# All eight tiles of u computed in pairs of seven products, in turn with the first gate pairs

## The chip, the core and the metric

The kernel runs on one core of one Trainium2 chip. The metric is device time in microseconds of one execution. The kernel before took 785.49 us in the median of three runs (784.92 to 785.92); its profiled execution took 785.08 us, of which the profile's span, from the first to the last instruction, is 783.3 us.

## What is computed

One layer of an encoder trunk on 512 tokens of width 1024, in float32. The change lies in the middle of the first half, in the three lines on u, on the spatial mix and on the two gates:

```python
q, k, v, g, u, sv, a_ret, a_sgu = jnp.split(proj, list(np.cumsum(IN_SPLITS)[:-1]), axis=-1)
y_ret = _retention_branch(q, k, v, g, ret_decay_logit, w_ret_o)      # (o * silu(g)) @ w_ret_o
u = jax.nn.gelu(u)
sv = _layernorm(jax.nn.gelu(sv), sgu_ln_g, sgu_ln_b)
mixed = jnp.einsum('gpq,bnqgc->bnpgc', w_spatial, svc) + b_spatial.T[None, None, :, :, None]
y = u * mixed.reshape(B, S, SGU_W)                                   # then y @ w_sgu_o
merged = jax.nn.sigmoid(a_ret) * y_ret + jax.nn.sigmoid(a_sgu) * y_sgu
```

`u` and the two gates are products of the normalised input (1024 x 512) with 1024 columns of `w_in` each, `y_ret` and `y_sgu` end in a product with another 1024 x 1024 matrix. Each is eight tiles of 128 features by 512 tokens.

## The kernel before

**Numbers.** A float32 operand is split into a high part (a ScalarE copy that rounds, `copy`, L97) and a low part (a VectorE subtraction, `split`, L116), and a product of two operands is three TensorE matmuls: high by high, high by low, low by high (`mm3`, L291 to L293).

**Whole tiles and pairs.** A tile of 128 features can be made by `f_block`: eight 128 x 128 weight blocks, three matmuls of 512 columns each, 24 in all, into one PSUM bank. Its weights are one unit of 1024 columns ("blk"). Two tiles can also be made together by `Pair`: the two feature tiles, the two halves of the inner dimension and the two halves of the tokens form a 2 x 2 by 2 x 2 block product, which takes seven half-sized products in place of eight. Each product is twelve matmuls of 256 columns (L917), so a pair takes 84. Its weights are seven forms: three of the raw blocks as they are (`B11`, `B21`, `B22`) and four sums (`T1` to `T4`, L198 to L204). Each form is split like a block and holds one of nine slots (`w4`); a whole tile's weights hold two. The raw weights come by DMA from SyncE's queue into four `raw` tiles; a pair holds three of them (two loads and one tile of sums) until its last forms are split.

**The three parts of a pair.** `part1` issues four products. The first goes to bank 0, and ScalarE copies it to the output tile; the second goes to bank 1 and VectorE adds it (L938); the third goes to bank 2; the fourth accumulates into bank 0, on top of the first, so it may start only when ScalarE's copy of the first product is done. `part2` is one product more into bank 0, which needs the next such copy done, and `part3` two, one into bank 0 and one into bank 2. Between the parts stand other matmuls, which cover the copies. `part3` ends with the scaling by `rbc` (L962, L967) and the activation (L963, L968).

**The stages around the change.** The SGU's normalised operand ends at about 199 us with `row_sums`. Then: four tiles of u by `f_block`, each scaled on VectorE (L979) and through gelu on ScalarE (L980), with the layer norm of sv beside them (`sv_stats`, `sv_scale`, `sv_norm`); two pairs of u (`UW` = 4 is the tile where the pairs begin); then four rounds `j` of one gate pair (sigmoid, `gated_pair`), two tiles of the retention's output by `f_block`, the gating product (L1051) into `r`, and two `mix`es. A mix is four 128 x 128 matmuls (L1011), an affine step (L1019) and the product with u (L1027) on VectorE, and the split of the result into `yh`, `yl`. After that come four rounds of the second gate, whose whole tiles read `yh` and `yl`, and then `w_out` and the feed-forward part, which the change leaves alone.

**Order.** Each engine runs its instructions in a fixed order. A scheduler sets it when the program is built, from the order of the source and from `issue_after`, which puts a block's instructions behind a named instruction on the same engine. `w_get` decides how far the weights run ahead: it fills units until eight or ten slots are spoken for.

Of the kernel before, what the change touches and what calls it, by code (L numbers as in the profile page):

```python
# [15 lines left out]
P = 128  # L16
# [11 lines left out]
SV0, U0, GATE0, GATE1 = 24, 32, 40, 72  # L28
UW = 4
LOOK = 4  # L30
# [8 lines left out]
EARLY = 4  # L39
QK = (4, 0, 5, 1, 6, 2, 7, 3)  # L40
COUPLES = [(i, i + 1) for i in range(4, 20, 2)]

# [7 lines left out]
def tile_block(ctx: ExitStack, tc, xT, x, wall, par, cs, wsp, bsp, gpost, gffn, out):  # L50
# [74 lines left out]
    while i < NW:  # L125
        pair = [(f, i) for f in FORMS]
        if i == SV0:
# [149 lines left out]
    def w_get(look=LOOK):  # L277
# [10 lines left out]
        return w_ready.pop(i)  # L288

    def mm3(o, ah, al, bh, bl, start, stop, skip=False):  # L290
        nc.tensor.matmul(o, ah, bh, start=start, stop=False, skip_group_check=skip)  # L291
        nc.tensor.matmul(o, ah, bl, start=False, stop=False, skip_group_check=skip)  # L292
        nc.tensor.matmul(o, al, bh, start=False, stop=stop, skip_group_check=skip)  # L293

# [605 lines left out]
    class Pair:  # L900
# [9 lines left out]
        def product(self, b, act, first, w=None):  # L910
            wh, wl = w or w_get()
            o = self.b[b][:, T0]
            for k in range(4):
                c = slice(k * P, (k + 1) * P)
                h_, l_ = act(k)
                for n, (w_, a_) in enumerate(((wh, h_), (wh, l_), (wl, h_))):
                    self.last = nc.tensor.matmul(  # L917
                        o, w_[:, c], a_, start=first and k == n == 0, stop=k == 3 and n == 2,
                        skip_group_check=True,
                    )  # L920
            return self.two(o)

# [33 lines left out]
        def part3(self):  # L956
# [4 lines left out]
            else:  # L961
                v.tensor_mul(two(c0[:, T1]), o, two(self.scale[:, T1]))  # L962
                nc.scalar.activation(out=c0, in_=c0, func=self.func)  # L963
            o = self.product(2, self.s("S4"), False, self.w[1])
            v.tensor_sub(two(c1[:, T0]), o, two(c1[:, T0]))
            if self.scale is not None:
                v.tensor_mul(c1, c1, self.scale)  # L967
                nc.scalar.activation(out=c1, in_=c1, func=self.func)  # L968


    bst = lo64("bst", F32)
    nc.gpsimd.dma_start(bst, bsp.rearrange("g p -> (g p)")[None, :].to_broadcast([P, S]))
    uT, late = [], None
    U_HOMES = [lambda: lo64("u", F32), lambda: hi192("u", F32)] + [lambda: blk(n="u")] * 2 + [lambda: hi192("u", F32)] * 4
    for j in range(UW):
        with tc.issue_after(summed) if j == 0 else ExitStack():
            o = f_block(xh, xl, KD)
        u = U_HOMES.pop()()
        i = v.tensor_mul(two(u), in_turn(o), two(rbc)).ins  # L979
        g = nc.scalar.activation(out=u, in_=u, func=AF.Gelu_apprx_tanh).ins  # L980
        uT.append(u)
        with tc.issue_after(i):
            sv_stats(((0, 1), (2, 3), (), ())[j])
        if j == 1:
            sv_scale()
        if j > 1:
            with tc.issue_after(g):
                sv_norm(j - 2, range((NT, 2)[j - 2]))
    for j in range(UW // 2, KD // 2):
        p = Pair(AF.Gelu_apprx_tanh, lambda: U_HOMES.pop()(), None, rbc)  # L990
        p.part1()
        if late:
            late.part3()
        p.part2()
        late = p
        uT += p.t
        if j == UW // 2:
            with tc.issue_after(p.copied):
                sv_norm(1, range(2, NT))
    yh, yl = [], []  # L1000

    def mix(j):
# [7 lines left out]
        for t in range(NT):  # L1010
            nc.tensor.matmul(  # L1011
                o[:, t * P : (t + 1) * P],
# [3 lines left out]
                stop=True,  # L1016
            )
        m = tmp("mix")
# [7 lines left out]
        )  # L1026
        v.tensor_mul(uT[j], m, uT[j])  # L1027
        h_, l_ = blk(F32R, "yh"), blk(F32R, "yl")
        split(h_, l_, uT[j])
# [3 lines left out]

    def gated_pair(ah, al, late=None):

        p = Pair(AF.Sigmoid, lambda: tmp("sig"), None, rbc)
        with tc.issue_after(late.last.ins) if late else ExitStack():
            p.part1()
        if late:
            with tc.issue_after(p.last.ins):  # L1040
                late.part3()
        o = [f_block(ah, al, KD)]
# [3 lines left out]

    r = []
    for j in range(KD // 2):
        for o, t in gated_pair(ogh, ogl, late if j == 0 else None):
            b = (lo64("r", F32) if j == 0 else hi192("r", F32) if j < 3 else blk(n="r"))  # L1050
            v.tensor_mul(two(b), in_turn(o), two(t))  # L1051
            r.append(b)
        mix(2 * j)
        mix(2 * j + 1)
    mh, ml = [], []
# [605 lines left out]
```

## Time and profile before

| What | Value |
|---|---|
| median of three runs | 785.49 us |
| profiled execution | 785.08 us |
| its span | 783.3 us |
| TensorE, mean granted clock | 0.998 |
| from the first matmul of u to the first of the second gate | 199.34 to 325.38 us |
| the same stretch, ScalarE busy | 63.53 us of 126.04 |
| one table load on ScalarE there | 1.28 us |

A row of the timeline gives the start, the duration, the engine, the source line, the operation with output and inputs, and how many alike were merged. Durations of TensorE overlap, since its matmuls are pipelined: what one costs is the distance to the next start. The chain of waits lists the pieces of work that ended last, one behind the other, so its pieces on TensorE do not overlap. On ScalarE and VectorE too the next instruction of a row of like ones starts some 0.1 us before the one ahead has ended.

### The profile page before, as it was taken

How to read it: one execution, taken by the hardware profiler on the slowest of the kernel's cores; microseconds unless marked ns; L12 is line 12 of the kernel's file. 1: busy time of each engine (PE TensorE's matmuls, PEld its weight loads, DVE VectorE, ACT ScalarE, POOL GpSimd, SP SyncE). 2: the span in 40 equal slices, each digit the busy share in tenths (PEclk: the TensorE clock that was granted, in tenths of full speed). 3: DMA queues.
4: the chain of work that ended last, by engine and by line, in shares of the span. 5: the costliest groups of instructions: out<-in, count | busy, mean ns of one | idle time of the engine just before them, and what ended most of it. 6: DMA issues, size and time to landing. Idle time of an engine off the chain costs nothing.

```text
span 783.3 us, 13258 instructions
## 1 busy us (share of the span) xinstructions
PE 775.6 (99%) x5067; PEld 720.3 (92%) x5067; DVE 626.5 (80%) x1067; ACT 467.8 (60%) x848; POOL 104.0 (13%) x132
## 2 busy tenths in 40 slices
PE   9999999999999999999999999999999999999996
PEld 8888998998899999999998998999999998999996
DVE  7467887788786877867765679989999889877987
ACT  7555558689385544444444776657777578644542
POOL 0040001130012111032211200001111012200001
PEclk9999999999999999999999999999999999999999
DMA  8782224453123333223459111425555365632244
GB/s 293 260 266 88 81 82 162 108 133 126 55 106 108 108 108 108 106 84 108 138 161 344 57 69 39 122 108 141 141 149 149 108 196 114 170 114 108 108 162 162
DMA packets 35889, 104.78 MB, mean 134 GB/s; under 512 B 4401, under 2 KB 6321, under 8 KB 35825
## 3 DMA queue, kind: packets, MB, share of 16 engines
q1 hardware_dynamic: 27936, 87.81, 31.8%
q0 software_dynamic: 7024, 14.95, 9.0%
q10 hardware_dynamic: 864, 1.18, 0.4%
q8 instruction: 39, 0.64, 0.3%
q14 instruction: 26, 0.20, 0.1%
HBM read 91.34 MB, written 4.19 MB: 122 GB/s over the span
## 4 chain that ended last, share of the span: by engine, by line
PE 98%; DVE 1%; ACT 0%; POOLq 0%; issue 0%; POOL 0%; DVEq 0%
PE ps L917 22%; PE ps L291 13%; PE ps L293 13%; PE ps L292 13%; PE ps L1354 11%; PE ps L746 5%; PE ps L625 4%; PE ps L627 4%; PE ps L626 4%; PE ps L1089 2%; PE ps L1091 2%; PE ps L1090 2%; PE ps L1370 2%; PE ps L1011 1%; PE ps L411 1%; PE ps L393 0%
## 5 line engine op out<-in xcount | busy, mean ns | idle before, releaser
L116 DVE TENSOR_TENSOR wl<-raw,wh 128x1024 fp32r<-128x1024 f32 (+1 forms) x88 | 100.6, 1152 | 56.1 <-issue 20.6
L97 ACT ACTIVATE wf<-raw 128x512 fp32r<-128x512 f32 x126 | 75.6, 624 | 83.8 <-PE ps L292 37.1
L97 ACT ACTIVATE wh<-raw 128x1024 fp32r<-128x1024 f32 (+2 forms) x92 | 89.1, 981 | 28.9 <-DMA raw<-wall 15.5
L917 PE MATMUL ps<-sh,wf 128*128 128x256 f32 x576 | 105.3, 275 | 0.0
L116 DVE TENSOR_TENSOR wf<-raw,wf 128x512 fp32r<-128x512 f32 x126 | 93.3, 754 | 14.9 <-ACT wf L97 14.7
L917 PEld LDWEIGHTS ps<-sh,wf 128*128 128x128 f32 x576 | 91.7, 192 | 0.8 <-ACT u L97 0.2
L291 PE MATMUL ps<-h2h,wh 128*128 128x512 f32 (+1 forms) x256 | 90.7, 354 | 0.0
L293 PE MATMUL ps<-h2h,wl 128*128 128x512 f32 (+1 forms) x256 | 90.4, 353 | 0.0
L292 PE MATMUL ps<-h2l,wh 128*128 128x512 f32 (+1 forms) x256 | 90.4, 353 | 0.0
L917 PE MATMUL ps<-sl,wf 128*128 128x256 f32 x288 | 79.3, 275 | 0.0
L1354 PE MATMUL ps<-dh,fh 128*128 128x256 f32 x216 | 59.5, 276 | 0.0
L1354 PE MATMUL ps<-dh,fl 128*128 128x256 f32 x216 | 59.5, 275 | 0.0
L1354 PE MATMUL ps<-dl,fh 128*128 128x256 f32 x216 | 59.4, 275 | 0.0
L917 PEld LDWEIGHTS ps<-sl,wf 128*128 128x128 f32 x288 | 55.3, 192 | 0.4
L97 ACT ACTIVATE dh<-raw 128x768 fp32r<-128x768 f32 (+1 forms) x36 | 33.6, 950 | 33.5 <-DVE raw L224 17.6
L293 PEld LDWEIGHTS ps<-h2h,wl 128*128 128x128 f32 x256 | 48.6, 190 | 5.1
L291 PEld LDWEIGHTS ps<-h2h,wh 128*128 128x128 f32 x256 | 48.7, 190 | 4.5
L292 PEld LDWEIGHTS ps<-h2l,wh 128*128 128x128 f32 x256 | 48.7, 190 | 4.4
L627 PE MATMUL ps<-wh,xl 128*128 128x512 f32 x128 | 48.6, 379 | 0.0
L626 PE MATMUL ps<-wl,xh 128*128 128x512 f32 x128 | 48.5, 379 | 0.0
L625 PE MATMUL ps<-wh,xh 128*128 128x512 f32 x128 | 48.5, 380 | 0.0
L917 PE MATMUL ps<-xh,wf 128*128 128x256 f32 x240 | 43.8, 276 | 0.0
(343 smaller groups left out, 2185.8 us busy)
## 6 DMA issues: line engine op xcount, KB each, us to landing
raw<-wall SPq DMA_DIRECT2D x144, 512.0 KB, 3.6
x<-x SPq DMA_DIRECT2D x24, 256.0 KB, 5.9
fl<-gp POOLq DMA_DIRECT2D x12, 256.0 KB, 4.0
swap<-qkraw POOLq DMA_DIRECT2D x16, 128.0 KB, 4.3
x<-x POOLq DMA_DIRECT2D x8, 256.0 KB, 2.3
fl<-fs POOLq DMA_DIRECT2D x8, 256.0 KB, 3.3
xT<-xT SPq DMA_DIRECT2D x7, 256.0 KB, 5.5
xT<-xT POOLq DMA_DIRECT2D x4, 256.0 KB, 4.0
```

Source lines behind the costliest of these rows:

```text
L97: return nc.scalar.activation(out=o, in_=i, func=AF.Copy)
L116: low[0] = nc.vector.tensor_sub(lo, src, as32(hi)).ins
L291: nc.tensor.matmul(o, ah, bh, start=start, stop=False, skip_group_check=skip)
L292: nc.tensor.matmul(o, ah, bl, start=False, stop=False, skip_group_check=skip)
L293: nc.tensor.matmul(o, al, bh, start=False, stop=stop, skip_group_check=skip)
L625: nc.tensor.matmul(acc[t], xh[k][:, c], turns(wh[:, f]), start=k == 0, stop=False)
L626: nc.tensor.matmul(acc[t], xh[k][:, c], turns(wl[:, f]), start=False, stop=False)
L627: part_end[0] = nc.tensor.matmul(acc[t], xl[k][:, c], turns(wh[:, f]), start=False, stop=k == KD - 1)
L746: nc.tensor.matmul(bank[t], a_[:, c], turns(w_[:, f]), start=first and k == i == 0, stop=last and k == 3 and i == 2, skip_group_check=True,)
L917: self.last = nc.tensor.matmul(o, w_[:, c], a_, start=first and k == n == 0, stop=k == 3 and n == 2, skip_group_check=True,)
L1089: nc.tensor.matmul(o, ah, turns(bh), start=k == 0, stop=False)
L1354: nc.tensor.matmul(o, a_[:, c], turns(w_[:, f]), start=j == t == i == 0, stop=j == DP - 1 and i == 2 and n not in (M2, M3, M4), skip_group ...
```

## The change

The four whole tiles of u become two more pairs, so that u is four pairs, and the order of the whole stretch is written out in a table, `MIDDLE`. In it `W` is a whole tile of the retention's output, `U1`, `U2`, `U3` and `G1`, `G2`, `G3` are the three parts of a pair of u and of a gate pair, `UA` and `GA` their activations, `M` a mix without its split, and `Y` the split. Each step is issued behind the last matmul of the step ahead.

```diff
-UW = 4
+MIDDLE = [(i[:-1], int(i[-1])) for i in (
+    "W0 W1 U10 W2 U20 G10 U30 G20 U11 G30 W3 UA0 GA0 M0 M1 U21 G11 Y0 Y1 U31 G21 U12 G31 W4 UA1 GA1 M2 M3 U22 G12"
+    " Y2 Y3 U32 W5 G22 U13 G32 W6 UA2 GA2 M4 M5 U23 G13 U33 W7 UA3 Y4 Y5 G23 M6 M7 G33 GA3 Y6 Y7"
+).split()]
...
-        elif U0 + UW <= i < GATE0:
-            units += pair
-            i += 2
+        elif i == U0:
+            us, gs = ([[(f, k + n * m) for f in FORMS] for n in range(KD // 2)] for k, m in ((U0, 2), (GATE0, 4)))
+            ws = [("blk", GATE0 + 4 * (n // 2) + 2 + n % 2) for n in range(KD)]
+            for what, n in MIDDLE:
+                units += {"W": lambda: ws[n : n + 1], "U1": lambda: us[n][:4], "U2": lambda: us[n][4:],
+                          "G1": lambda: gs[n][:4], "G2": lambda: gs[n][4:]}.get(what, list)()
+            i = GATE0 + 2 * KD
...
                 v.tensor_mul(two(c0[:, T1]), o, two(self.scale[:, T1]))
-                nc.scalar.activation(out=c0, in_=c0, func=self.func)
+                if self.func:
+                    nc.scalar.activation(out=c0, in_=c0, func=self.func)
...
         v.tensor_mul(uT[j], m, uT[j])
+
+    def mixed(j):
         h_, l_ = blk(F32R, "yh"), blk(F32R, "yl")
         split(h_, l_, uT[j])
...
+    def whole(n):
+        o = f_block(ogh, ogl, KD)
+        r.append(lo64("r", F32) if n < 3 else hi192("r", F32) if n == 3 else blk(n="r"))
+        done = copy(two(r[n]), in_turn(o)).ins
+        if n < 2:
+            with tc.issue_after(low[0]):
+                sv_stats(((0, 1), (2, 3))[n])
+                if n:
+                    sv_scale()
+        if 0 < n < 5:
+            with tc.issue_after(done):
+                sv_norm((n - 1) // 2, range(NT)[:2] if n % 2 else range(NT)[2:])
+
+    def u_first(n):
+        us[n] = Pair(None, lambda: hi192("u", F32), None, rbc)
+        us[n].part1()
+
+    def u_acts(n):
+        for i, t in enumerate(us[n].t):
+            nc.scalar.activation(out=t, in_=t, func=AF.Gelu_apprx_tanh)
+            uT[2 * n + i] = t
+
+    def g_first(n):
+        gs[n] = Pair(None, lambda: tmp("sig"), None, rbc)
+        gs[n].part1()
+
+    def g_acts(n):
+        for i, t in enumerate(gs[n].t):
+            nc.scalar.activation(out=t, in_=t, func=AF.Sigmoid)
+            v.tensor_mul(r[2 * n + i], r[2 * n + i], t)
...
+    pe_last[0] = summed
+    for what, n in MIDDLE:
+        with tc.issue_after(pe_last[0]):
+            does[what](n)
```

A whole tile of the retention's output is now copied to `r` by ScalarE as it is, and the gate is multiplied in later, from SBUF. The second gate's pairs keep their old form. In the weights' layout all of u is now stored as pairs.

How the change moves instructions is shown at three places, in each engine's own order. The numbers in a name tell buffers apart: the last of them is the tile's own. In the changed kernel the same source lines have other numbers (L97 has become L100, L116 L119, L962 L972, L967 L978, L1019 L1005).

**ScalarE where a pair of u begins.** Before, the second pair of u (`ps_483_2484` is its bank 0). Its first copy is the last row here:

```order
L97 ACTIVATE u_467_2380<-ps_468_2381 128x256
L717 ACTIVATE sv_383_1912<-sv_383_1912,sshift_776,srstd_775 128x512
L97 ACTIVATE wf_476_2453<-raw_472_2400 128x512
L717 ACTIVATE sv_384_1913<-sv_384_1913,sshift_776,srstd_775 128x512
L97 ACTIVATE u_467_2380<-ps_468_2381 128x256
L97 ACTIVATE wf_477_2470<-raw_462_2343 128x512
L97 ACTIVATE wf_480_2477<-raw_478_2473 128x512
L97 ACTIVATE u_481_2482<-ps_483_2484 128x256
```

Of the change, the second pair (`ps_492_2567` is its bank 0, step `U11`):

```order
L1052 ACTIVATE u_455_2301<-u_455_2301 128x512
L100 ACTIVATE sig_477_2442<-ps_478_2443 128x256
L100 ACTIVATE wf_488_2558<-raw_473_2434 128x512
L1052 ACTIVATE u_456_2302<-u_456_2302 128x512
L100 ACTIVATE wf_489_2562<-raw_482_2462 128x512
L100 ACTIVATE u_490_2565<-ps_492_2567 128x256
```

The first copy of the new pair now stands behind both gelus of the pair before (`u_455_2301`, `u_456_2302`), and those wait for VectorE's scaling of that pair.

**ScalarE where the second gate begins.** Before, the last sigmoid of the first gate, and the first copy of the first pair of the second (`ps_637_3535` is its bank 0):

```order
L968 ACTIVATE sig_601_3310<-sig_601_3310 128x512
L97 ACTIVATE wf_621_3444<-raw_613_3385 128x512
L97 ACTIVATE wf_640_3538<-raw_610_3362 128x512
L97 ACTIVATE yh_628_3515<-u_481_2482 128x512
L97 ACTIVATE sig_635_3533<-ps_637_3535 128x256
```

Of the change (`ps_647_3667` is that bank):

```order
L100 ACTIVATE wf_634_3603<-raw_621_3491 128x512
L100 ACTIVATE yh_641_3657<-u_585_3248 128x512
L100 ACTIVATE wf_650_3670<-raw_618_3457 128x512
L1061 ACT_TABLE_LOAD
L1061 ACTIVATE sig_611_3435<-sig_611_3435 128x512
L100 ACTIVATE yh_643_3661<-u_586_3249 128x512
L1061 ACTIVATE sig_612_3436<-sig_612_3436 128x512
L100 ACTIVATE sig_645_3665<-ps_647_3667 128x256
```

A table load, both sigmoids of the last gate pair (`GA3`) and two splits of mixes have come directly ahead of that copy.

**VectorE at the same place.** Before, from the gating product of the last round to the addition in the second gate's first pair (L938):

```order
L1051 TENSOR_TENSOR r_624_3503<-ps_622_3447,sig_601_3310 128x512
L116 TENSOR_TENSOR wf_621_3444<-raw_613_3385,wf_621_3444 128x512
L1019 SCALAR_TENSOR_TENSOR mix_627_3512<-ps_626_3507,part_63,add_625_3505 128x512
L1005 SCALAR_TENSOR_TENSOR add_630_3519<-rws_382_1911,part_63,bst_443_2205 128x128
L1027 TENSOR_TENSOR u_481_2482<-mix_627_3512,u_481_2482 128x512
L1019 SCALAR_TENSOR_TENSOR mix_632_3526<-ps_631_3521,part_63,add_630_3519 128x512
L116 TENSOR_TENSOR wf_640_3538<-raw_610_3362,wf_640_3538 128x512
L116 TENSOR_TENSOR yl_629_3516<-u_481_2482,yh_628_3515 128x512
L1027 TENSOR_TENSOR u_482_2483<-mix_632_3526,u_482_2483 128x512
L938 TENSOR_TENSOR sig_635_3533<-ps_638_3536,sig_635_3533 128x256
```

Of the change, up to the scaling that the second sigmoid waits for (L978):

```order
L119 TENSOR_TENSOR wf_633_3599<-raw_617_3456,wf_633_3599 128x512
L1005 SCALAR_TENSOR_TENSOR mix_637_3613<-ps_636_3608,part_63,add_635_3606 128x512
L991 SCALAR_TENSOR_TENSOR add_638_3616<-rws_382_1911,part_63,bst_444_2213 128x128
L1013 TENSOR_TENSOR u_585_3248<-mix_637_3613,u_585_3248 128x512
L119 TENSOR_TENSOR wf_634_3603<-raw_621_3491,wf_634_3603 128x512
L1005 SCALAR_TENSOR_TENSOR mix_640_3623<-ps_639_3618,part_63,add_638_3616 128x512
L972 TENSOR_TENSOR sig_611_3435<-ps_613_3437,rbc_103_567 128x256
L1013 TENSOR_TENSOR u_586_3249<-mix_640_3623,u_586_3249 128x512
L976 TENSOR_TENSOR sig_612_3436<-ps_615_3439,sig_612_3436 128x256
L119 TENSOR_TENSOR yl_642_3658<-u_585_3248,yh_641_3657 128x512
L978 TENSOR_TENSOR sig_612_3436<-sig_612_3436,rbc_103_567 128x512
```

Ahead of them stand the low part of the first whole tile of the second gate (`wl_632_3582`), two splits of mixes (`yl_627_3572`, `yl_629_3576`) and a 128 x 256 subtraction (L963). The scalings of the last gate pair (L972, L976, L978) were done before the mixes in the old order, and now stand between and behind them.

More of the change, by code (lines that the diff above doesn't have):

```diff
@@ L920, in product @@
                     )
+            pe_last[0] = self.last.ins
             return self.two(o)
@@ L967, in part3 @@
                 v.tensor_mul(c1, c1, self.scale)
-                nc.scalar.activation(out=c1, in_=c1, func=self.func)
+                if self.func:
+                    nc.scalar.activation(out=c1, in_=c1, func=self.func)
     bst = lo64("bst", F32)
     nc.gpsimd.dma_start(bst, bsp.rearrange("g p -> (g p)")[None, :].to_broadcast([P, S]))
[L973 to L999, printed above, removed]
+    uT = {}
     yh, yl = [], []
@@ L1031, in mix, with gated_pair @@
         yl.append(l_)
-    def gated_pair(ah, al, late=None):
+    def gated_pair(ah, al):
         p = Pair(AF.Sigmoid, lambda: tmp("sig"), None, rbc)
[L1037 to L1041, printed above, removed]
+        p.part1()
         o = [f_block(ah, al, KD)]
@@ L1045, in gated_pair @@
         return zip(o, p.t)
[L1047 to L1054, printed above, removed]
+    r, us, gs = [], {}, {}
+    def whole(n):
[24 more added lines that the diff above has]
+            v.tensor_mul(r[2 * n + i], r[2 * n + i], t)
+    does = {
+        "W": whole, "M": mix, "U1": u_first, "Y": mixed, "U2": lambda n: us[n].part2(), "U3": lambda n: us[n].part3(),
+        "UA": u_acts,
+        "G1": g_first, "G2": lambda n: gs[n].part2(), "G3": lambda n: gs[n].part3(), "GA": g_acts,
+    }
+    pe_last[0] = summed
+    for what, n in MIDDLE:
+        with tc.issue_after(pe_last[0]):
+            does[what](n)
     mh, ml = [], []
```

9 lines of the change are left out of this document (5 added, 4 removed).

## The prediction

> **What bounds the kernel now.** First the page's busy shares and the engines' shares of the chain that ended last, then the stretch that the change rewrites and a denser one, as windows (busy us of PE, PEld, DVE, ACT, POOL, then clock, DMA share, GB/s).
>
> ```profile
> PE 775.6 (99%) x5067; PEld 720.3 (92%) x5067; DVE 626.5 (80%) x1067; ACT 467.8 (60%) x848; POOL 104.0 (13%) x132
> ...
> PE 98%; DVE 1%; ACT 0%; POOLq 0%; issue 0%; POOL 0%; DVEq 0%
> ...
> 199.34:325.38 126.04, 126.01 (x859) 118.17 (x858) 96.12 (x161) 63.53 (x109) 17.87 (x13) 1.00 0.27 96
> ...
> 470.00:765.00 295.00, 295.00 (x2103) 279.32 (x2102) 261.43 (x423) 184.64 (x312) 25.38 (x30) 1.00 0.43 128
> ```
>
> TensorE is the end: 98% of the chain, busy 126.01 of 126.04 us in the stretch at the full clock. So the time falls by the TensorE work taken out, plus what it waits now, less what it will wait. A busy PE hides short waits under the tails of its matmuls, so they are read from starts, and the prices of TensorE's steps from the chain of waits, whose pieces do not overlap (start, us, what):
>
> ```profile
> 176.13 5.18 PE ps L746 x24
> 259.02 1.78 PE ps L1011 x16
> 325.38 5.36 PE ps L917 x48
> 694.60 9.38 PE ps L1354 x84
> ```
>
> 24 matmuls of 512 columns take 5.18 us: a whole tile. 84 of 256 columns take 9.38: a pair; 48 of them 5.36, so one product of twelve is 1.34. Two mixes take 1.78.
>
> **The sum of TensorE's work.** Four whole tiles of u go: 4 x 5.18 = 20.72 us. Two pairs come: 2 x 9.38 = 18.76. That is 1.96 us less. Everything else on TensorE is moved.
>
> **What it waits now.** The stretch holds twelve whole tiles, six pairs and eight mixes: 62.16 + 56.28 + 7.12 = 125.56 us, and lasts 126.04. So 0.48 us are waits. The largest is visible where the first pair's fourth product begins:
>
> ```profile
> 225.64 0.39 PE L917 MATMUL ps<-xh,wf 128*128 128x256 f32 x2
> 226.06 0.38 PE L917 MATMUL ps<-sh,wf 128*128 128x256 f32 x1
> ...
> 225.62 0.38 ACT L97 ACTIVATE u<-ps 128x256 f32<-128x256 f32 x1 [0.65 <-PE ps L917]
> ```
>
> Two matmuls of 0.11 us should be followed at 225.86; the next starts at 226.06, 0.06 us after ScalarE's copy of the bank has ended (226.00). The changed order without a wait is 8 x 5.18 + 8 x 9.38 + 7.12 = 123.60 us, 2.44 less than now. That is the most that can be won. What is to be found is how much it will wait.
>
> **Work moved at no cost.** The first step, W0, reads the retention's operand, where u read the input. Its last low part was ready at 195.78, before 199.34; if it came later, W0 would be late by as much.
>
> ```profile
> 195.10 0.68 DVE L116 TENSOR_TENSOR gl<-ps,gh 128x512 fp32r<-128x512 f32 x1
> ...
> raw<-wall SPq DMA_DIRECT2D x144, 512.0 KB, 3.6
> ```
>
> Pairs in turn share four raw tiles of weights, so a pair's loads on SyncE's queue wait until the pair ahead has split its sums. The slots set that: with nine, the slot that the first form of U1 takes is free six products, 8.0 us, ahead of its use, and a load of 3.6 us, two splits and a sum (0.6 each) fit. The number of loads stays. Without this cover each pair would wait for the rest of 3.6 us.
>
> **VectorE's and ScalarE's prices.** A run of rows on VectorE, whose distances are prices, and four on ScalarE:
>
> ```profile
> 260.93 0.74 DVE L1019 SCALAR_TENSOR_TENSOR mix<-ps,part,add 128x512 f32<-128x512 f32 x1
> 261.59 0.34 DVE L1005 SCALAR_TENSOR_TENSOR add<-rws,part,bst 128x128 f32<-128x128 f32 x1
> 261.85 0.68 DVE L1027 TENSOR_TENSOR u<-mix,u 128x512 f32<-128x512 f32 x1
> 262.45 0.74 DVE L1019 SCALAR_TENSOR_TENSOR mix<-ps,part,add 128x512 f32<-128x512 f32 x1
> 263.12 0.68 DVE L116 TENSOR_TENSOR wf<-raw,wf 128x512 fp32r<-128x512 f32 x1
> ...
> 264.92 0.42 DVE L938 TENSOR_TENSOR sig<-ps,sig 128x256 f32<-128x256 f32 x1
> 265.25 0.68 DVE L116 TENSOR_TENSOR yl<-u,yh 128x512 fp32r<-128x512 f32 x1
> 265.85 1.22 DVE L116 TENSOR_TENSOR wl<-raw,wh 128x1024 fp32r<-128x1024 f32 x1
> 266.99 0.69 DVE L116 TENSOR_TENSOR wf<-raw,wf 128x512 fp32r<-128x512 f32 x1
> ...
> 256.52 0.63 ACT L97 ACTIVATE wf<-raw 128x512 fp32r<-128x512 f32 x1 [4.00 <-PE ps L917]
> 257.17 1.28 ACT L963 ACT_TABLE_LOAD   x1
> 258.46 0.63 ACT L963 ACTIVATE sig<-sig 128x512 f32<-128x512 f32 x1
> 259.00 0.61 ACT L968 ACTIVATE sig<-sig 128x512 f32<-128x512 f32 x1
> ...
> 273.00 1.05 ACT L97 ACTIVATE wh<-raw 128x1024 fp32r<-128x1024 f32 x1
> ```
>
> VectorE: mix 0.66, its small step 0.26, 512 columns 0.60, 256 columns 0.33, a block's low part 1.14. ScalarE: 512 columns 0.54, a block 1.05, a table load 1.29. Sums over the stretch: VectorE loses 4 x (1.14 + 0.60) = 7.0 us and gains per pair eleven of 512 (seven splits, four sums) and an evacuation of 5 x 0.33 + 0.60, 8.9, so 17.7 for two; 96.1 + 10.7 = 107 of 123.6 us, 86%. ScalarE gains six table loads (7.7), eight copies of `r` (at most 8 x 0.63 = 5.0), and 14 form splits and six bank copies for four block splits (14 x 0.54 + 6 x 0.38 - 4 x 1.05 = 5.6): about 82 us, 66%. The 470 to 765 us stretch runs VectorE at 88.6% and loses nothing on TensorE. So the averages fit, and waits come only where a copy that TensorE needs stands behind others on ScalarE: the first copy of a pair, wanted when its third product ends, 3 x 1.34 = 4.02 us after the pair's start.
>
> **Where U1 begins.** That copy stands behind the gelus of U0, and the second gelu behind VectorE's scaling. From the end of W2: split of G0's third sum 0.63 + 0.60, the load that takes its raw tile 3.6, its high part 0.63 (5.46); VectorE from there six of 512, four of 256, a block and the scaling, 3.60 + 1.32 + 1.14 + 0.68 (12.20); gelu 0.54, split 0.54, copy 0.38, start 0.06 (13.72). TensorE has U20, G10, U30, G20 and three products ahead, eleven products, 14.74. Slack 1.0. But G0's sums on GpSimd run alongside, and such a one stretches a row:
>
> ```profile
> 230.45 1.72 POOL L201 TENSOR_TENSOR raw<-raw,raw 128x512 f32<-128x512 f32 x1 [14.01 <-DVE wf L116]
> ...
> 230.98 1.74 DVE L116 TENSOR_TENSOR wf<-raw,wf 128x512 fp32r<-128x512 f32 x1
> ```
>
> 1.74 where 0.69 is usual: 1.05 more takes the slack. Bounds 0 and 1.05 (a second stretch); I take 0.2, nearer to the row chain. For the other five entries inside the stretch, where norms, gelus or block splits stand ahead, another 0.2 together.
>
> **Where the second gate begins.** Here nothing covers. ScalarE's copy stands behind a table load, both last sigmoids and the splits of the last mixes; the second sigmoid waits for VectorE's scaling. From the end of W7, which frees the slots for the next block: its high part 1.05; VectorE the low part 1.14, seven of 512 (two splits of mixes, two forms, two products with u, one split) 4.20, two mixes and a small step 1.58, three of 256 0.99, the scaling 0.68: 9.64. Sigmoid 0.54, copy 0.38, start 0.06: 10.62, with some 0.2 for three hand-overs (0.06 each by the row at 226.06) 10.8. TensorE meanwhile has G23, two mixes, G33 and three products, six products and 1.78, 9.82, and three matmuls of a whole tile that the new order puts ahead of the fourth product, 0.65: 10.47. It waits 0.3. Queued behind that copy are the next block and forms, wanted later. Below, 0 if VectorE has run ahead; above, 1.4 with one stretched row.
>
> The waits are 0.2 + 0.2 + 0.3 = 0.7 us, the stretch 124.3, 1.74 less. The profiled span becomes 783.3 - 1.74 = 781.56; with the 1.78 us around it 783.34; the median stands 0.41 above that execution: **783.8 us**.
>
> **What the notes add.** Row: the split ahead of the table load ends at 257.15, the first sigmoid starts at 258.46, 1.31 us later. The Trainium skill, ScalarE: Activation LUTs, section "What ACT_TABLE_LOAD costs", puts about 1.28 us on the load, as here, and 1.38 of drain on top, and its rules for authors say to finish one set of functions before switching; this change does the opposite, seven switches for one. The row shows no drain. By the page's 2.66 my sum would be about 785, the second rival.
>
> **The rivals.**
>
> *Nothing waits* (0.07). The copies are all in time: 785.49 - 2.44 = 783.05. For it, 470 to 765 us; against it, the first pair's wait at 226.06.
>
> *A switch of tables costs more than its row, and ScalarE becomes late* (0.13). A load that also empties the pipeline, as long again as the row, is 1.3 us more. At the second gate ScalarE has 0.3 us to spare before the last sigmoid: u is ready for its split at 1.05 + 1.14 + 4 x 0.60 + 0.33 + 0.92 + 0.08 = 5.92, and four of 0.54 and the load make 9.37 against 9.64. So 1.0 more is seen there, and some 0.4 at U2, where a load stands ahead of two gelus: 785.2. For it, six new loads; against it, 1.31 us by the rows.
>
> *VectorE falls behind* (0.18), the one that ends slower. Eight GpSimd sums of the first gate each stretch a row by 1.05, 8.4 us, and the pairs in turn leave VectorE 86% full ahead of that. Each of seven entries can absorb about 0.5: 8.4 - 3.5 + 0.3 = 5.2 us of waits, 785.49 - 2.44 + 5.2 = 788.2. It decides from 2.4 us of waits, and is measurable from 4.0. For it, the row of 1.74; against it, that the same eight sums run now and the stretch waits 0.48 in all.
>
> **How the numbers follow.** My forecast, waits of 0.2 to 1.3 us, 783.2 to 784.4, has 0.62. A measurement tells 0.2%, 1.57 us, from no change: below 783.92 is faster. Of the forecast 0.43 lies there (waits under 0.87), with nothing waits 0.50; the other 0.19 and the tables make 0.32 the same; VectorE 0.18 slower. The range 782.9 to 786.6 holds the forecast, both smaller rivals and the lower end of the third; some 0.15 is left out, nearly all above.
>
> **What would show it.** Right: the stretch from `row_sums` to the second gate's first product about 124.3 us; 84 matmuls of each new pair 9.38 apart from waits; a gap of some 0.3 us at the fourth product of the second gate's first pair, released by ScalarE's copy; VectorE near 107 us busy. Wrong: gaps at every pair's fourth product (VectorE behind), more than 1.5 us between a ScalarE row and the sigmoid behind a table load, gaps with a DMA as releaser, or a difference outside the stretch, which I put at nothing.

## The result, and the profile after

The changed kernel took 783.59 us in the median of 16 runs (782.82 to 784.33), the kernel before beside it 785.08 (784.61 to 787.58, 16 runs). The ratio is 0.9978 with a 95% interval of 0.9972 to 0.9985: 1.49 us less, which lies about at the bound of 0.2% (1.57 us). The change was run twice more as it is: 783.57 and 783.55 us, 0.9982 [0.9973, 0.9991] and 0.9977 [0.9967, 0.9986]. One execution each of three kernels below (a2_again, e4_tail, e6_both) took over 1000 us and is left out of every number; that of e6_both was the profiled one, so its gaps are not read.

The page of the changed kernel, busy shares and the engines' shares of the chain that ended last, and the rewritten stretch as a window (busy us of PE, PEld, DVE, ACT, POOL, then clock, DMA share, GB/s):

```profile
PE 774.5 (99%) x5139; PEld 720.7 (92%) x5139; DVE 639.5 (82%) x1093; ACT 485.2 (62%) x878; POOL 103.5 (13%) x132
...
PE 92%; DVE 3%; DMA 3%; issue 1%; ACT 0%; POOLq 0%; DVEq 0%; POOL 0%; ACTq 0%
```

```profile
199.84:323.86 124.02, 124.02 (x931) 118.71 (x930) 106.54 (x181) 78.32 (x134) 17.88 (x13) 1.00 0.31 99
```

VectorE has gone from 96.12 to 106.54 us busy in it, and TensorE is still the engine that is never out of work. Like the window in the prediction, this one runs too far, here by 0.16 us: its end is a start from the chain of waits, which names this piece 0.16 us later than the timeline. So the stretch is measured with both ends from the chain.

The chain of waits of the changed kernel through the stretch (start, us, what):

```profile
199.53 0.47 PE ps L848 x2
...
210.36 5.36 PE ps L926 x48
...
220.90 18.76 PE ps L926 x168
...
246.62 19.00 PE ps L926 x168
...
321.18 6.71 PE ps L926 x60
327.92 0.29 issue
328.21 0.37 ACT sig L100
328.62 1.60 PE ps L926 x12
```

168 matmuls of 256 columns, two pairs' worth, last 18.76 us: twice the 9.38 of before. The second such piece lasts 19.00, so 0.24 us of waiting is in it. The other wait stands at the second gate's fourth product (the last row), where the chain goes through a piece of ScalarE; its length is read from starts below. The first pair of u and the second (steps U10 and U11) stand without a gap.

W0 begins at 199.53 + 0.47 = 200.00. The piece at 321.18 holds 24 matmuls of G33 and 36 of the second gate, which so begins at 321.18 + 24 x 0.112 = 323.86: 123.86 us. In the chain of before the two `row_sums` stand as

```profile
199.04 0.46 PE ps L839 x2
```

W0 there begins at 199.50 or 199.51, and the second gate at 325.38: 125.87 us. So from `row_sums` through the `part1` of the second gate's first pair the trace gains 2.01 - 0.36 = 1.65 us. These two profiled executions themselves, 785.08 and 784.33, differ by less: in this one W0 begins 0.50 us later (199.84 for 199.34), set by transfers in the first 7 us, and there are 0.84 us of gaps behind 665 us, where that of before has 0.06. In the two repeats W0 began at 199.41 and 199.26, and the late gaps were 0.22 and 0.47. These late gaps do not follow the order: of the kernels below, e2_new_order_whole, e4_tail and e5_entry have the new order and no such gap, and e9_old_order_no_norm has the old order and 0.65 us of them.

**The wait at the second gate**, ScalarE's timeline of the changed kernel (start, us, engine, line, operation):

```profile
324.48 0.61 ACT L100 ACTIVATE wf<-raw 128x512 fp32r<-128x512 f32 x1
325.11 1.28 ACT L1061 ACT_TABLE_LOAD   x1
326.40 0.64 ACT L1061 ACTIVATE sig<-sig 128x512 f32<-128x512 f32 x1
326.94 0.61 ACT L100 ACTIVATE yh<-u 128x512 fp32r<-128x512 f32 x1
327.67 0.64 ACT L1061 ACTIVATE sig<-sig 128x512 f32<-128x512 f32 x1
328.21 0.36 ACT L100 ACTIVATE sig<-ps 128x256 f32<-128x256 f32 x1
```

and VectorE's scaling that the second sigmoid waits for:

```profile
326.95 0.69 DVE L978 TENSOR_TENSOR sig<-sig,rbc 128x512 f32<-128x512 f32 x1
```

and TensorE, from the last matmul ahead to the second of the fourth product:

```profile
328.15 0.38 PE L302 MATMUL ps<-yh,wl 128*128 128x512 f32 x1
328.62 0.38 PE L926 MATMUL ps<-sh,wf 128*128 128x256 f32 x1
328.84 0.28 PE L926 MATMUL ps<-sl,wf 128*128 128x256 f32 x1
```

The scaling ends at 327.64, the sigmoid starts at 327.67, the copy ends at 328.57, the fourth product starts at 328.62. TensorE was free for it at 328.37, 0.22 behind the start of a matmul of 512 columns, so 0.25 are waited. The second matmul starts 0.22 behind the first instead of 0.11: a wait costs its length and 0.1 us more.

**The wait at the third pair of u** (step U12), ScalarE again, then VectorE, then TensorE at its third and fourth products:

```profile
257.03 1.28 ACT L1052 ACT_TABLE_LOAD   x1
258.32 0.64 ACT L1052 ACTIVATE u<-u 128x512 f32<-128x512 f32 x1
258.86 0.37 ACT L100 ACTIVATE sig<-ps 128x256 f32<-128x256 f32 x1
259.12 0.62 ACT L100 ACTIVATE wf<-raw 128x512 fp32r<-128x512 f32 x1
259.70 0.63 ACT L1052 ACTIVATE u<-u 128x512 f32<-128x512 f32 x1
260.38 0.63 ACT L100 ACTIVATE wf<-raw 128x512 fp32r<-128x512 f32 x1
260.92 0.37 ACT L100 ACTIVATE u<-ps 128x256 f32<-128x256 f32 x1
```

```profile
258.98 0.68 DVE L978 TENSOR_TENSOR u<-u,rbc 128x512 f32<-128x512 f32 x1
```

```profile
261.09 0.63 PE L926 MATMUL ps<-sh,wf 128*128 128x256 f32 x2
261.55 0.28 PE L926 MATMUL ps<-sl,wf 128*128 128x256 f32 x1
```

The same pattern: VectorE's scaling ends at 259.66, the second gelu starts at 259.70, and the copy, wanted at 261.20, is done at 261.29. The fourth product's second matmul starts at 261.55 instead of 261.31: 0.24 us in all.

### The profile page after: what moved, and what is told of

Same layout as the page of the kernel before. It is cut to its first block, busy times and chain, and to the rows that moved or that the text cites. A ratio compares the mean times of both kernels' runs of the same rounds, so it can differ in the third digit from the quotient of the medians.

```text
span 782.6 us, 13472 instructions
## 1 busy us (share of the span) xinstructions
PE 774.5 (99%) x5139; PEld 720.7 (92%) x5139; DVE 639.5 (82%) x1093; ACT 485.2 (62%) x878; POOL 103.5 (13%) x132
## 4 chain that ended last, share of the span: by engine, by line
PE 92%; DVE 3%; DMA 3%; issue 1%; ACT 0%; POOLq 0%; DVEq 0%; POOL 0%; ACTq 0%
PE ps L926 24%; PE ps L300 12%; PE ps L302 12%; PE ps L301 12%; PE ps L1372 7%; PE ps L755 5%; PE ps L634 4%; PE ps L636 4%; PE ps L635 4%; DMA raw<-wall 3%; PE ps L1109 2%; PE ps L1108 2%; PE ps L1107 2%; DVE dl L119 1%; PE ps L997 1%
## 5 line engine op out<-in xcount | busy, mean ns | idle before, releaser
L119 DVE TENSOR_TENSOR wl<-raw,wh 128x1024 fp32r<-128x1024 f32 (+1 forms) x84 | 96.0, 1152 | 54.3 <-issue 19.1
L100 ACT ACTIVATE wf<-raw 128x512 fp32r<-128x512 f32 x140 | 85.6, 625 | 67.3 <-PE ps L301 19.4
L926 PE MATMUL ps<-sh,wf 128*128 128x256 f32 x640 | 117.4, 276 | 0.1
L119 DVE TENSOR_TENSOR wf<-raw,wf 128x512 fp32r<-128x512 f32 x140 | 107.0, 774 | 9.2 <-ACT wf L100 8.6
L926 PEld LDWEIGHTS ps<-sh,wf 128*128 128x128 f32 x640 | 101.9, 192 | 1.1 <-ACT sig L100 0.5
L100 ACT ACTIVATE wh<-raw 128x1024 fp32r<-128x1024 f32 (+2 forms) x88 | 84.8, 977 | 28.5 <-DMA raw<-wall 14.0
L926 PE MATMUL ps<-sl,wf 128*128 128x256 f32 x320 | 88.0, 275 | 0.0
L926 PEld LDWEIGHTS ps<-sl,wf 128*128 128x128 f32 x320 | 61.4, 192 | 0.4
L100 ACT ACTIVATE dh<-raw 128x768 fp32r<-128x768 f32 (+1 forms) x36 | 33.6, 950 | 33.8 <-DVE raw L231 15.2
L926 PE MATMUL ps<-xh,wf 128*128 128x256 f32 x288 | 52.2, 275 | 0.0
```

The costliest lines, as they stand in the source:

```text
L100: return nc.scalar.activation(out=o, in_=i, func=AF.Copy)
L119: low[0] = nc.vector.tensor_sub(lo, src, as32(hi)).ins
L926: self.last = nc.tensor.matmul(o, w_[:, c], a_, start=first and k == n == 0, stop=k == 3 and n == 2, skip_group_check=True,)
```

## The experiments

All are compared with runs of the kernel before on the same chip. "Gaps" are the starts of TensorE's matmuls that come late, from the first matmul behind `row_sums` to the end of the second gate's first `part1`, in one profile of each; before has 0.30. The 0.08 us by which the matmul behind two mixes comes late is in the mixes' 1.78 us and not counted.

| run | median us (n) | ratio to before [95%] | difference, us | gaps, us |
|---|---|---|---|---|
| the change | 783.59 (16) | 0.9978 [0.9972, 0.9985] | -1.49 | 0.60 |
| a1_again, the change | 783.57 (11) | 0.9982 [0.9973, 0.9991] | -1.46 | 0.49 |
| a2_again, the change | 783.55 (10) | 0.9977 [0.9967, 0.9986] | -1.69 | 0.85 |
| e1_pairs_old_order | 787.97 (5) | 1.0037 [1.0023, 1.0051] | +2.94 | 4.88 |
| e2_new_order_whole | 785.27 (11) | 1.0002 [0.9994, 1.0011] | +0.24 | 0.36 |
| e3_one_table | 783.00 (8) | 0.9974 [0.9964, 0.9984] | -2.03 | 0.05 |
| e4_tail | 783.27 (7) | 0.9971 [0.9960, 0.9981] | -2.11 | 0.32 |
| e5_entry | 783.46 (9) | 0.9975 [0.9965, 0.9985] | -1.92 | 0.62 |
| e6_both | 783.40 (7) | 0.9970 [0.9959, 0.9980] | -1.98 | not read |
| e6_again | 783.25 (6) | 0.9970 [0.9958, 0.9981] | -1.99 | 0.22 |
| e7_sums_on_vector | 783.22 (7) | 0.9974 [0.9964, 0.9985] | -2.16 | 0.37 |
| e8_tail_and_sums | 782.97 (5) | 0.9968 [0.9956, 0.9981] | -2.27 | 0 |
| e9_old_order_no_norm | 784.02 (11) | 0.9981 [0.9972, 0.9989] | -1.22 | 1.48 |

The intervals of e4_tail to e8_tail_and_sums overlap those of the change: what these runs show are the gaps and not a difference in time.

### The change again

No edit.

> The changed kernel once more, unaltered. Its first profiled execution began its stretch 0.66 us later than the one of before (200.00 against 199.34) and lost 0.84 us in gaps between 665 and 770 us, where the one of before lost 0.06. Theory: both are of that one execution (arrival of transfers), not of the change: the stretch lasts 123.9 us again up to the second gate, gaps of some 0.24 at the fourth product of U2 and 0.36 at the fourth product of the second gate's first pair stand again, and the gaps behind 665 us are different, 0 to 0.9. Rival: the changed stretch shifts or rearranges the later loads, and the same gaps of 0.8 us stand behind 665 us again.

Measured: 783.57 us, span 781.7; the late gaps 0.22 us for the 0.84 of the first profile. The stretch repeats: 0.12 at the third pair of u, 0.37 at the second gate. What lies outside it varies with the execution.

### The pairs without the new order

```diff
-UW = 4
+UW = 0
...
+        with tc.issue_after(p.sum if j < 2 else p.copied):
+            if j < 2:
+                sv_stats(((0, 1), (2, 3))[j])
+            else:
+                sv_norm(j - 2)
```

All of u as four pairs, one behind the other, in the old place; the gate keeps its old order. The layer norm of sv, which stood beside the four whole tiles, now stands beside the pairs.

> The kernel before with all of u in pairs, in its old order (four pairs of u, one behind the other). Theory: the seven products take 1.96 us off TensorE in any order, but in this one VectorE has 8.9 us of work for each 9.38 of TensorE, with 5.3 us of statistics on top, so some of it is waited for: between 1.5 us faster and 1 us slower than before, with gaps in the first 40 us of the stretch. Rival (the order does nothing): 1.7 to 2.2 us faster, as the change or better.

Measured: 2.94 us slower than before, where my theory ended at +1; that the seven products bring their gain in any order has fallen. Windows of this kernel, columns as above: the 30 us ahead of a stall, the first 1.33 us behind it, and the 3 us after that.

```profile
199.00:228.80 29.80, 29.77 (x265) 29.52 (x264) 28.90 (x59) 19.22 (x38) 1.96 (x3) 1.00 0.29 95
...
231.67:233.00 1.33, 1.33 (x10) 1.33 (x11) 1.33 (x3) 0.99 (x2) 1.15 (x1) 0.86 0.39 136
233.00:236.00 3.00, 3.00 (x16) 3.00 (x16) 3.00 (x5) 1.60 (x3) 0.45 (x1) 0.50 0.31 120
```

The timeline of TensorE there (the bracket is the idle time and what ended it), of ScalarE (ahead of its rows a window, columns as above, in which it never pauses), and of VectorE:

```profile
228.70 0.28 PE L917 MATMUL ps<-sh,wf 128*128 128x256 f32 x1
231.67 0.38 PE L917 MATMUL ps<-sh,wf 128*128 128x256 f32 x1 [2.70 <-ACT u L97]
```

```profile
224.50:231.62 7.12, 4.47 (x41) 4.28 (x39) 6.14 (x12) 7.12 (x14) 0.00 (x0) 1.00 0.23 74
...
228.46 0.81 ACT L717 ACTIVATE sv<-sv,sshift,srstd 128x512 f32<-128x512 f32 x1
229.17 1.14 ACT L97 ACTIVATE wf<-raw 128x512 fp32r<-128x512 f32 x2
230.21 0.62 ACT L968 ACTIVATE u<-u 128x512 f32<-128x512 f32 x1
230.73 0.62 ACT L97 ACTIVATE wf<-raw 128x512 fp32r<-128x512 f32 x1
231.25 0.37 ACT L97 ACTIVATE u<-ps 128x256 f32<-128x256 f32 x1
```

```profile
228.72 0.69 DVE L967 TENSOR_TENSOR u<-u,rbc 128x512 f32<-128x512 f32 x1
```

VectorE is busy 28.90 of 29.80 us, 97%, and has fallen behind: the scaling of a pair ends at 229.41, after the third product of the next has ended its starts. ScalarE has fallen behind too: from 224.50 to 231.62 it is never idle, with four normalisations of sv in its queue (L717, the last at 228.46), and the gelu that the scaling had made ready at 229.41 starts only at 230.21, with a split and the first copy behind it. The fourth product comes 2.86 us late; by these rows some 0.8 of it is ScalarE's queue alone (an estimate: 230.21 less 229.41). Behind the stall the granted clock falls to 0.50, and the 24 matmuls from 231.67 to 236.08 take 4.41 us instead of 2.68. The sum, 4.88 us of gaps (0.29 at the first pair's fourth product, then 2.86 and 1.73) less the 0.30 of before and less 1.96 of work saved, is +2.6 of the +2.94 us.

### The same with the norm left out

```diff
-        with tc.issue_after(p.sum if j < 2 else p.copied):
-            if j < 2:
-                sv_stats(((0, 1), (2, 3))[j])
-            else:
-                sv_norm(j - 2)
-        if j == 1:
-            sv_scale()
```

This kernel leaves out the layer norm of sv. It asks whether the wait comes from the crowd on VectorE and ScalarE, or from pairs that stand back to back.

> All of u in pairs in the old order, and the layer norm of sv left out (its statistics, their scale and the normalising), which frees some 5.5 us of VectorE and 5.8 us of ScalarE in the first 40 us of the stretch. Theory: the wait of 2.86 us that the old order showed came from VectorE being full there (28.9 of 29.8 us) and from the norms ahead of the copies on ScalarE; without them it falls to 0.5 us or less, the clock does not fall, and the kernel is 1.2 to 2.2 us faster than before. Rival (pairs one behind the other wait in any case, by their own copies): 0 to 3 us slower than before again.

Measured: 784.02 us, 1.22 less than before. The same two places, the window and TensorE's timeline:

```profile
199.00:228.80 29.80, 29.77 (x265) 29.50 (x264) 26.86 (x49) 18.38 (x37) 0.00 (x0) 1.00 0.33 110
```

```profile
229.99 0.38 PE L917 MATMUL ps<-sh,wf 128*128 128x256 f32 x1 [0.72 <-ACT u L97]
```

With VectorE at 90% the wait is 0.89 us, and the clock stays at 1.00. So the norm's work beside the pairs makes 1.97 of the 2.86 us and with it the fall of the clock. How much of that is the statistics on VectorE and how much the normalisations on ScalarE this run does not tell, since it leaves out both. The rest remains, more than the 0.5 that I had expected.

### The new order without the pairs

The table `MIDDLE` stays, but the first four tiles of u are whole tiles again, in the steps U1 and U3 of the first two pairs:

```diff
+                if what[0] == "U" and n < 2:
+                    units += {"U1": [("blk", U0 + 2 * n)], "U3": [("blk", U0 + 2 * n + 1)]}.get(what, [])
+                    continue
```

> The changed kernel with the first four tiles of u as whole tiles again, in the new order: U10 and U30, U11 and U31 are one whole tile each. Theory: TensorE's work is that of before, 125.56 us in the stretch, with 0.3 to 0.6 us of waits: within 0.4 us of before, and 1.2 to 2.0 slower than the change. Rival (the new order is what brings the time): 1 us or more faster than before.

Measured: 785.27 us, no different from before, with 0.36 us of gaps at the second gate alone. The order has no gain of its own. Of the two orders only the new one lets the pairs bring theirs: order alone +0.24, pairs alone +2.94, both -1.46 on the same chip.

### One activation table

```diff
-            nc.scalar.activation(out=t, in_=t, func=AF.Gelu_apprx_tanh)
+            nc.scalar.activation(out=t, in_=t, func=AF.Sigmoid)
```

On u a sigmoid takes the place of gelu, so that gelu is left out and six of seven table loads go.

> The changed kernel with sigmoid in place of gelu on u, which leaves gelu out: the six more table loads fall away, 7.7 us of ScalarE. Theory: they stand beside TensorE, and the last copy waits for VectorE's scaling, not for the load: 0 to 0.4 us faster than the change. Rival (a switch costs 1.3 us of TensorE, or 2.7 with a drain): 3 us or more faster.

Measured: 783.00 us (782.55 to 783.28), 0.57 below the change on the same chip (783.35 to 783.96), a little more than I had expected, and the two ranges do not meet; of the 0.49 us of gaps 0.05 are left. A switch that cost 1.3 us more than its row at both late places would have shown as more. But the scheduler also placed the copy differently at the second gate, as ScalarE's timeline shows, so there the two causes are not told apart:

```profile
325.59 0.37 ACT L100 ACTIVATE sig<-ps 128x256 f32<-128x256 f32 x1
...
327.32 0.63 ACT L1061 ACTIVATE sig<-sig 128x512 f32<-128x512 f32 x1
```

### The last sigmoids behind the copy

```diff
-    " Y2 Y3 U32 W5 G22 U13 G32 W6 UA2 GA2 M4 M5 U23 G13 U33 W7 UA3 Y4 Y5 G23 M6 M7 G33 GA3 Y6 Y7"
+    " Y2 Y3 U32 W5 G22 U13 G32 W6 UA2 GA2 M4 M5 U23 G13 U33 W7 UA3 Y4 Y5 G23 M6 M7 G33 Y6 Y7"
...
         p.part1()
+        if between:
+            with tc.issue_after(p.copied):
+                between()
...
-        for i, (o, t) in enumerate(gated_pair(yh, yl)):
+        for i, (o, t) in enumerate(gated_pair(yh, yl, (lambda: g_acts(3)) if j == 0 else None)):
```

> The changed kernel with the last gate pair's sigmoids (GA3) moved behind the first two copies of the second gate's first pair. Theory: that copy now waits for nothing late, so the gap of 0.36 us (0.25 and 0.11) at the second gate's fourth product goes, the one of 0.12 to 0.24 at the fourth product of U2 stays: 0.2 to 0.5 us faster than the change, 783.2. Rival: VectorE is late as such, and the wait only moves to the next copy or to the whole tile that reads the last mixes: within 0.1 us of the change.

Measured: the gap at the second gate is gone, that at the third pair of u stays (0.32). ScalarE's timeline, then the chain of waits:

```profile
324.70 0.38 ACT L100 ACTIVATE sig<-ps 128x256 f32<-128x256 f32 x1
...
329.12 1.28 ACT L1064 ACT_TABLE_LOAD   x1
```

```profile
320.64 8.04 PE ps L926 x72
```

The copy is 3.5 us earlier and the table load 4 us later (2.9 and 4.6 counted from each kernel's W0), and 72 matmuls stand in one piece. That wait was the copy's place in ScalarE's queue, and nothing else is late behind it.

### The gelus behind the copy

```diff
-    "W0 W1 U10 W2 U20 G10 U30 G20 U11 G30 W3 UA0 GA0 M0 M1 U21 G11 Y0 Y1 U31 G21 U12 G31 W4 UA1 GA1 M2 M3 U22 G12"
-    " Y2 Y3 U32 W5 G22 U13 G32 W6 UA2 GA2 M4 M5 U23 G13 U33 W7 UA3 Y4 Y5 G23 M6 M7 G33 GA3 Y6 Y7"
+    "W0 W1 U10 W2 U20 G10 U30 G20 U11 G30 W3 GA0 M0 M1 U21 G11 Y0 Y1 U31 G21 U12 G31 W4 GA1 M2 M3 U22 G12"
+    " Y2 Y3 U32 W5 G22 U13 G32 W6 GA2 M4 M5 U23 G13 U33 W7 UA3 Y4 Y5 G23 M6 M7 G33 GA3 Y6 Y7"
...
         us[n].part1()
+        if n:
+            with tc.issue_after(us[n].copied):
+                u_acts(n - 1)
```

> The changed kernel with the gelus of a pair of u put behind the first two copies of the next pair of u on ScalarE; the number of table loads stays at seven. Theory: the gap at the fourth product of U2 (0.12 to 0.24 us) goes, the one of 0.36 at the second gate stays: 0.1 to 0.3 us faster than the change. Rival: the mixes that read these gelus become late and the time comes back there: no difference or slower.

Measured: the gap at 261 is gone, and one of 0.27 stands at 255.41, one step earlier, at G21 (a gate pair's `part2`, which waits for a copy too). The wait has moved, though not to the mixes, as the rival had it. ScalarE's timeline there:

```profile
254.24 0.63 ACT L100 ACTIVATE wf<-raw 128x512 fp32r<-128x512 f32 x1 [1.52 <-DVE raw L208]
254.78 0.36 ACT L100 ACTIVATE sig<-ps 128x256 f32<-128x256 f32 x1
```

The copy stands behind a form's split, and that waits for a sum on VectorE (L208, `T2`). The change has the same order here, but its sum starts 0.41 us earlier counted from W0, and its three profiles wait 0, 0 and 0.11 us. So at this place VectorE itself is late, and reordering ScalarE does not take the wait away. VectorE's 0.4 us begin at a split that lasts 1.77 us in this kernel and 1.48 in the change, both times beside a GpSimd sum.

### Both moves

The two edits above together, twice.

> Both moves together. Theory: no gap over 0.05 us between the first step W0 and the second gate, the stretch lasts 123.6 us, and the kernel takes 0.5 us less than the change, 783.0, 2.0 to 2.4 less than before. Rival (new waits take their place): 783.4 or more.

> Both moves of ScalarE's sigmoids and gelus together, once more, since the profile of the first try cannot be read (its core ran at a clock of 0.752). Theory: the gap at the second gate is gone; those around 255 to 261 us are 0 to 0.3; the time is 0.2 to 0.6 us below the change. Rival: the waits stand elsewhere, and the time is that of the change within 0.1.

Measured: 783.40 and 783.25 us. In the profile of e6_again only 0.22 us at 256.14, at G21, is left, where I had expected of e6_both that none would be.

### GpSimd's sums on VectorE

```diff
-            eng = nc.vector if i < GATE0 or i >= UP0 else nc.gpsimd
+            eng = nc.vector if i < GATE1 - 16 or i >= UP0 else nc.gpsimd
```

at both sums, `T2` and `T4`, for the first gate's four pairs.

> The changed kernel with the eight sums of the first gate's forms (T2, T4) on VectorE instead of GpSimd: 8 x 0.60 = 4.8 us more for VectorE, and no row stretched by GpSimd. Theory: VectorE is the engine that is late at the two gaps, so its work counts there: they stay or grow, 0 to 0.8 us slower than the change. Rival (GpSimd's stretching is what makes VectorE late): the gaps shrink and it is 0.3 us or more faster.

Measured: 783.22 us, and the gap at the third pair of u is gone; that at the second gate stays (0.37). I had expected VectorE, with eight sums of 0.60 us more, to be later. The window of this kernel, to be held against the one of the same length in the section on the result:

```profile
199.67:323.69 124.02, 124.02 (x933) 118.86 (x932) 105.53 (x189) 78.49 (x135) 4.99 (x5) 1.00 0.32 100
```

VectorE has eight instructions more and is 1.01 us less busy. The groups say why (line, shapes, count, then busy us and mean ns); first the change, then this kernel:

```profile
L119 DVE TENSOR_TENSOR wf<-raw,wf 128x512 fp32r<-128x512 f32 x59 | 45.3, 775 | 5.0 <-ACT wf L100 4.8
...
L206 DVE TENSOR_TENSOR raw<-raw,raw 128x512 f32<-128x512 f32 x8 | 6.6, 823 | 2.3 <-DMA raw<-wall 2.3
```

```profile
L119 DVE TENSOR_TENSOR wf<-raw,wf 128x512 fp32r<-128x512 f32 x59 | 41.0, 702 | 5.0 <-ACT wf L100 4.7
...
L206 DVE TENSOR_TENSOR raw<-raw,raw 128x512 f32<-128x512 f32 x8 | 5.5, 688 | 2.8 <-DMA raw<-wall 2.8
```

The same 59 splits take 4.3 us less and the same 8 sums 1.1: GpSimd's sums had stretched VectorE's rows by more than the sums cost on VectorE. The timeline of the change has seven VectorE rows of 512 columns that last 1.11 to 1.77 us instead of 0.69. Each of them ends 0.55 us behind the end of a GpSimd sum; six are gone here, the seventh stands beside a sum that stayed on GpSimd. One of the six is a split at 245.38 (1.48 us): behind it VectorE has no pause up to the scaling that the third pair's copy waits for, and here, counted from W0, that scaling starts 0.77 us earlier. So the wait at the third pair was VectorE's lateness from this.

### The tail and the sums

The edits of e4_tail and e7_sums_on_vector together; and the change again beside it.

> The changed kernel with the last gate pair's sigmoids behind the second gate's first copies, and the first gate's eight sums on VectorE. Each of the two alone left one gap. Theory: together none over 0.05 us is left between W0 and the second gate's fourth product, the stretch lasts 123.6 us, and the time is 0.3 to 0.7 us below the change. Rival: VectorE's 4.8 us more bring a new gap.

> The changed kernel a third time, beside the three below on one chip. Theory: 1.0 to 2.2 us faster than before, 0.3 to 0.7 us of gaps up to the second gate's fourth product, and gaps behind 665 us that differ once more from 0.84 and 0.22. Rival: the same gaps behind 665 us as in the first profile.

Measured: 782.97 us and, on the same chip, 783.55 for the change (W0 at 199.26, gaps of 0.11 at 255.49, 0.39 at 261.24, 0.35 at the second gate). The chain of e8_tail_and_sums has whole pieces at both places:

```profile
246.73 18.76 PE ps L926 x168
...
321.05 8.04 PE ps L926 x72
```

No start is late by 0.05 us or more, the step behind the mixes apart. The stretch lasts 123.63 us by the chain (200.10 to 321.05 + 2.68). This version has the lowest median of all that leave nothing out, and is faster than the kernel before by 2.27 us. Against the change the medians differ by 0.58, but the intervals overlap, and the difference in time is not shown; that the gaps are gone is.

## Why the prediction was right

783.8 us was forecast, 783.59 measured, faster as forecast. By its steps:

- **TensorE's work, -1.96.** Right. Pairs last 9.38 us, two of them 18.76, and the gap-free stretch of e8_tail_and_sums lasts 123.63 us where the sum was 123.60.
- **It waits 0.48 now; at most 2.44 can be won.** Mis-sized by 0.17, by a reading error of mine: 199.34 was a start from the timeline and 325.38 one from the chain. With both from the chain before lasts 125.87 us, 0.31 more than its sum of 125.56, and the late starts add up to 0.30. The most to be won was 2.27.
- **W0's operand and the four shared raw tiles, nothing.** Right. W0 follows the two `row_sums` at 199.37 and 199.61 at their own distance (199.84), and no gap of TensorE in the stretch has a DMA as releaser.
- **VectorE 107, ScalarE about 82.** 106.54 and 78.32: the first met, the second 4 too high, which changed nothing: the seventh table load and the last two sigmoids lie behind the window, and a copy of `r` lasts 0.58 and not 0.63.
- **The wait of 0.2 where U1 begins, 0.2 at the other five entries.** The sum of the right size, the places not. U11 has no gap in any of the three profiles of the change. The third pair has 0.24, 0.12 and 0.39, and in one profile G21 has 0.11: 0.24, 0.12 and 0.50 for my 0.4. The cause that I had named for U1, a VectorE row stretched by a GpSimd sum, is the one that e7_sums_on_vector showed, but at the third pair. That the two figures of 0.2 come near the sum is in part luck.
- **The wait of 0.3 at the second gate.** Right in place, mechanism and size: 0.36, 0.37 and 0.35, released by ScalarE's copy behind the sigmoid behind VectorE's scaling; taking that order away (e4_tail) took the wait away. VectorE's run from the block's low part (319.02) through that scaling (327.64) holds the rows that my sum had, and lasts 8.62 us for 8.59. The 0.1 that each wait also costs at the matmul behind it was not in my sum, which by its parts had 0.33.
- **The waits together, 0.7.** 0.60, 0.49 and 0.85.
- **Nothing outside the stretch.** Not shown wrong, but -1.74 was forecast and the three comparisons gave -1.49, -1.46 and -1.69. Work saved and gaps (-1.96 - 0.30 + 0.60, and so on) add up to -1.66, -1.77 and -1.41 for the three profiles. Their spans lie 0.76, 1.65 and 0.88 us below that of before. The rest stands at three places outside the stretch: W0's start (0.50 later, 0.07 later, 0.08 earlier), gaps near 505 us (0.37 before; 0, 0.31 and 0.58 after) and the late gaps (0.06 before; 0.84, 0.22 and 0.47). With these the three sums are -0.75, -1.6 and -0.9, so nothing is missing. One profile of before cannot tell whether these places differ on average, so of the medians 0.1 to 0.3 us are not placed.

**Nothing waits** was a limit that the change missed by 0.5 to 0.85 us; with two more moves it is reached. **The dearer table switch** did not come: the split ahead of the load ends at 325.09 and the sigmoid starts at 326.40, 1.31 us, the distance of before, and without six switches 0.57 us are gained. The Trainium skill (ScalarE: Activation LUTs, "What ACT_TABLE_LOAD costs") counts 1.38 us of drain on top; no row here shows it, and the load's own 1.28 is as it says. **VectorE falls behind** did not come in this order, where it is 86% busy. In the old order, with the norm beside the pairs, VectorE at 97% did fall behind, and ScalarE with it. GpSimd's stretching, the mechanism of this rival, is in the change too: 5.4 us in the two groups shown, where I had put 8.4. What I held against it, that the same sums already ran before, was weak: before, three rows were stretched, in the change seven. The order left enough room for nearly all of it.

## What to carry to other kernels

A scheme that saves products loads the engines that prepare operands; its gain is real only where the work around it is arranged so that no window fills them, and in this kernel the same saving was worth -1.5 us in one order and +2.9 in another. A copy that the bounding engine waits for should not stand in a queue behind an activation that waits for a third engine. Before a helper's work is left on a second engine because the first is busy, look at whether the rows of the first get longer beside it.

## What the hardware showed that was not expected

**A short stall cost more than half again.** In e1_pairs_old_order TensorE was idle for 2.70 us; the granted clock was 0.86 in the 1.33 us behind it and 0.50 in the next 3.00, and the matmuls stood 0.21 us apart instead of 0.11: 1.73 us on top of a wait of 2.86. All five executions seem to have it: their mean granted clock is 0.994 to 0.996, where the kernel before has 0.997 to 0.999. In e9_old_order_no_norm an idle time of 0.72 us brought no such fall. The Trainium skill (TensorE: Matmul & The Clock Gate, "What's actually happening") has the clock halve after an idle window of about 3.4 us; here 2.70 us were enough. A window from 232.60 to 232.90 has a clock of 0.55 and one from 236.00 to 237.00 has 0.98, so the slow time began 1.0 us after TensorE had resumed and lasted 3.4 us, which fits that window's length.

**A sum on GpSimd cost VectorE more than it saved.** Eight sums moved to VectorE left it 1.01 us less busy in the stretch. The Trainium skill (SBUF — State Buffer, "Who interferes with whom") says that a VectorE instruction with two inputs in SBUF and a GpSimd instruction that reads SBUF exclude each other; the row of 1.74 us in the prediction, which ends 0.55 behind the GpSimd sum's end, agrees, and so do the seven of the change.
